# The conditioning stage of a hybrid decoder layer: two row tiles of h per step, 1 KB packets, a ring of weight tiles

## The chip, the cores and the metric

The kernel runs on one core of a Trainium2 chip. The metric is the device time of one execution in microseconds (us). Three runs of the kernel before took 1973.09, 1976.62 and 1977.78 us; the median is 1976.62 us. The engines in the text are PE (TensorE, matrix products; its weight loads are a row of their own, PEld), DVE (VectorE), ACT (ScalarE), POOL (GpSimd) and SP (SyncE), which issues nearly all DMAs here.

## The reference

One decoder layer on x of shape (1024, 2048), in float32. What matters for the change is its beginning:

```
shift, scale, gate = split(silu(c) @ w_ada + b_ada)      # c: (2048,), w_ada: (2048, 6144)
h    = x * (1 + scale) + shift                           # (1024, 2048)
proj = h @ w_in                                          # w_in: (2048, 7184)
... retention (4 heads), gated DeltaNet (8 heads), mixed @ w_out, gate, LayerNorm
```

The first two thirds of w_ada (33.5 MB) and all of x (8.4 MB) have to be read before the last row tile of h exists. The product with w_in is the first large one.

## The kernel before

h is kept transposed, as 16 row tiles (index kt) of 128 channels by 1024 tokens, each split into a high part h_hi and a low part h_lo, both in a reduced float32 format that PE takes at full rate. A product of h and w_in is three products: high by high, low by high, high by low.

The first stage, the conditioning stage, makes the 16 row tiles and does the first of the products meanwhile. It runs in steps s_ (lines 332 to 372). In a step, for row tile kt = s_:

- `load_w` (L188) loads the columns of shift and scale that belong to kt: four tiles `wa` of 256 KB twice, where each packet is 128 floats, 512 bytes. `load_x` (L184) loads the 128 channels of x, also in 512-byte packets.
- `accumulate` (L196) multiplies row r of each partition by silu(c) and adds it up on DVE, 14 rows of 256 elements (shift and scale side by side) into two accumulators that are added at the end (L205). The last two rows are left to PE.
- `reduce` (L207), in the next step, sums over the partitions with PE: products one column wide with the accumulator and the two rows that are left over. DVE adds the bias (`mod`, L219).
- `transpose_x` (L229) turns x on PE in two groups of four transposes, and ACT copies them out of PSUM.
- `modulate` (L216): ACT scales and shifts (L223), ACT rounds to h_hi (L224), DVE subtracts to get h_lo (L227).
- `load_item`, `split_item`, `first_mms` (L243, L266, L277): an item is one row tile of w_in with the columns of a group (0 or 1). It is loaded, split into w_hi (ACT, L274) and w_lo (DVE, L275) and multiplied in three units t = 0, 1, 2. A unit is six products 512 wide (L291), except unit 2 of group 0, six products 272 wide (L286). There are 32 items, 96 units.

A planner (L313 to L328) puts the units into steps and slots. It takes the items in the order of `TURNS` (L142): row tiles 0 to 3 of group 0, 0 to 7 of group 1, 4 to 11 of group 0, 8 to 15 of group 1, 12 to 15 of group 0. A unit of the newest row tile may not stand before slot `LATE`; a step has `SLOTS` slots, a unit counts one slot (0.6 for the short kind), and what does not fit goes to the next step. All engines follow this written order in the stage (`manual_schedule`), and each queue, SP's too, runs strictly in order. When a group's turn ends, its three sums are evicted from PSUM to SBUF, by ACT the first time (L306) and by DVE as an addition later (L308).

Behind the stage come the other products with w_in (`gemm_v`, L489, is the first, `gemm_cm`, L457, the most) with the heads' work between them, and at the end the product with w_out.

Of the kernel before, what the change touches and what calls it, by code (L numbers as in the profile page):

```python
# [58 lines left out]
def hybrid_layer_kernel(ctx: ExitStack, tc: tile.TileContext, x, c, w_ada, b_ada, w_in, gdn_conv_w,  # L59
# [86 lines left out]
    part_g, part_k, part_q0, part_k0, part_g0 = (pa.tile([P, T], F32, name=f"part{i}", tag=f"part{i}")  # L146
                                                 for i in range(5))
    part_v = pa.tile([P, 2, DV + 16], F32, name="part5", tag="part5")
    parts = ((part_g, part_k, part_v), (part_q0, part_k0, part_g0))
    hH, hL = [], []  # L150
    with ExitStack() as st:
# [8 lines left out]
        def load_params():  # L160
            prm = sp.tile([P, P], F32, name="prm", tag="acc", bufs=4)
            nc.sync.dma_start(out=prm[:96], in_=gdn_conv_w[0].rearrange("j (t p) -> (j t) p", p=P))
            nc.sync.dma_start(out=prm[96:128], in_=b_ada[0, :2 * D].rearrange("(t p) -> t p", p=P))
            prm2 = sp.tile([32, P], F32, name="prm2", tag="acc", bufs=4)
# [15 lines left out]
        NV = 14  # L180
        NS = 4
        xss, xTs, accs, was, raws, splits = {}, {}, {}, {}, {}, {}

        def load_x(kt):  # L184
            xss[kt] = sp.tile([P, NC, P], F32, name="xs", tag="xs")
            nc.sync.dma_start(out=xss[kt], in_=x3[:, :, kt * P:(kt + 1) * P])

        def load_w(kt, rhs=range(4)):  # L188
            for rh in rhs:
                wa = sp.tile([P, 4, 2, P], F32, name="wa", tag="wa", bufs=7)  # L190
                for s in range(2):
                    nc.sync.dma_start(out=wa[:, :, s, :], in_=ada3[:, rh * 4:rh * 4 + 4,
                                                                  s * D + kt * P:s * D + (kt + 1) * P])
                was.setdefault(kt, []).append(wa)

        def accumulate(kt, r0, r1):  # L196
            if r0 == 0:
                accs[kt] = [sp.tile([P, 2 * P], F32, name="acc", tag="acc", bufs=4) for _ in range(2)]
            for r in range(r0, r1):
                wr, a = was[kt][r // 4][:, r % 4].rearrange("p s n -> p (s n)"), accs[kt][r % 2]  # L200
                V.scalar_tensor_tensor(out=a, in0=wr, scalar=cs[:, r:r + 1],  # L201
                                       in1=zero.broadcast_to([P, 2 * P]) if r < 2 else a, op0=ALU.mult, op1=ALU.add)
            if r1 == NV:
                a, b = accs[kt]
                V.scalar_tensor_tensor(out=a, in0=a, scalar=1.0, in1=b, op0=ALU.mult, op1=ALU.add)  # L205

        def reduce(kt):  # L207
            a, _ = accs.pop(kt)
            pm = px.tile([P, 512], F32, name="px", tag="px")
            for s in range(2):  # L210
                for r in range(NV, 16):
                    PE.matmul(pm[:, s:s + 1], was[kt][r // 4][:, r % 4, s], cs[:, r:r + 1], start=r == NV, stop=False)
                PE.matmul(pm[:, s:s + 1], a[:, s * P:(s + 1) * P], ones[:, 0:1], start=False, stop=True)
            return pm

        def modulate(kt, pm):  # L216
            xT = xTs.pop(kt)
            mod = sp.tile([P, 2], F32, name="mod", tag="mod")
            V.tensor_tensor(out=mod, in0=pm[:, 0:2], in1=bcol[:, kt], op=ALU.add)  # L219
# [3 lines left out]
            S.activation(out=xT, in_=xT, func=AF.Identity, scale=mod[:, 1:2], bias=mod[:, 0:1])  # L223
# [5 lines left out]
        def transpose_x(kt, i):  # L229
            if i == 0:  # L230
                xTs[kt] = sp.tile([P, T], F32, name="xT", tag="xT")
            ph = px.tile([P, 512], F32, name="px", tag="px")
            for j in range(4):
                PE.transpose(ph[:, j * P:(j + 1) * P], xss[kt][:, 4 * i + j], ident)
            S.copy(xTs[kt][:, i * 512:(i + 1) * 512], ph)
# [7 lines left out]
        def load_item(n):  # L243
# [7 lines left out]
            if grp == 2:  # L251
                r3 = raw[:, :2 * (DV + 16)].rearrange("p (a n) -> p a n", n=DV + 16)
                nc.sync.dma_start(out=r3[:, :, :DV], in_=w3[:, 0:2, RV:RV + DV])
                nc.sync.dma_start(out=r3[:, :, DV:], in_=w3[:, 0:2, GA:GA + 16])
                cols = ()
            elif grp == 0:
                cols = ((RG + P, P), (GK, P), (RV, DV), (GA, 16))
            else:
                cols = ((RQ, P), (RK, P), (RG, P))
# [53 lines left out]
        todo = [(n, t) for n in range(len(items) - 1) for t in range(3)]  # L313
        plan = []
        for s_ in range(KT + 1):
            plan.append([])
            at = 0.0
            while todo and s_:
                n, t = todo[0]
                grp, kt = items[n][:2]  # L320
                if kt == s_ - 1:
                    at = max(at, LATE)
                if kt > s_ - 1 or (s_ < KT and at > SLOTS - 1 + 0.2):
# [5 lines left out]
        load_w(0, range(1))  # L329
        load_x(0)  # L330
        prm = load_params()
        for s_ in range(KT + 1):
            if s_ < KT:
                load_w(s_, range(0 if s_ else 1, 4))
                if s_ < KT - 1:
                    load_x(s_ + 1)
            for n in ((0,), (1, 2))[s_] if s_ < 2 else ():
                load_item(n)
# [4 lines left out]
            if s_ < KT:  # L343
# [5 lines left out]
            if 1 <= s_ <= 3:  # L349
                h_rest()  # L350
            h_rest = None
            for i in range(max([SLOTS] + [e[0] + 1 for e in plan[s_]])):
# [18 lines left out]
                if i == LATE - 1 and h_rest:  # L371
                    h_rest()
# [858 lines left out]
```

## Time and profile before

| | us |
|---|---|
| median of three runs | 1976.62 |
| the profiled execution | 1977.74 |
| its span, from the first to the last instruction | 1976.0 |
| PE busy in the span | 1890.5 (96%) |
| DVE busy | 1154.2 (58%) |
| ACT busy | 554.6 (28%) |
| the first product behind the stage (L489) starts at | 211.76 |

PE's time is busy nearly throughout; the slices in which it is not are at the start. A busy share says nothing of the clock: the granted clock of a stretch (PEclk, 1.00 for 2.4 GHz throughout) stands beside it in the windows. The share of the DMA engines in a stretch can go over 1, since packets overlap.

### The profile page before, as it was taken

What the parts mean: (1) busy time and instruction counts of PE and PEld (TensorE: products, weight loads), DVE (VectorE), ACT (ScalarE), POOL (GpSimd) and SP (SyncE); (2) the same over time, 40 slices, a digit from 0 to 9 for tenths busy, and PEclk for the clock granted to TensorE, in tenths of its full rate; (3) what the DMA queues carried; (4) which work ended last, traced back from release to release, by engine and by line L of the source; (5) the groups of instructions that cost most, each with busy time, mean ns of one, the idle gap of its engine ahead of it and who ended that gap; (6) DMA issues with size and microseconds to landing.
All of it is one profiled execution on the core that took longest, in us unless ns stands there. A gap on an engine that the chain in (4) does not pass through costs nothing.

```text
span 1976.0 us, 28123 instructions
## 1 busy us (share of the span) xinstructions
PE 1890.5 (96%) x10400; PEld 1595.4 (81%) x10400; DVE 1154.2 (58%) x2953; ACT 554.6 (28%) x1243; POOL 168.4 (9%) x165
## 2 busy tenths in 40 slices
PE   5989999999999999999999999999999999998996
PEld 4768888787878888787878898898898878886885
DVE  6767657564765757574665752544542534458557
ACT  3443223332322232322323221211211232234221
POOL 0000101000000000000000000100100100005102
PEclk8999999999999999999999999999999999999998
DMA  9998312222222222221222241144141166345532
GB/s 259 281 255 215 95 54 72 54 73 54 68 59 58 60 57 67 54 71 50 72 54 58 63 139 48 43 145 134 38 139 49 55 209 221 123 136 186 180 112 91
DMA packets 292459, 210.07 MB, mean 106 GB/s; under 512 B 44681, under 2 KB 252122, under 8 KB 291554
## 3 DMA queue, kind: packets, MB, share of 16 engines
q1 hardware_dynamic: 289698, 199.89, 36.1%
q0 software_dynamic: 2624, 8.39, 1.2%
q8 instruction: 81, 1.33, 0.3%
q14 instruction: 56, 0.46, 0.1%
HBM read 189.31 MB, written 18.92 MB: 105 GB/s over the span
## 4 chain that ended last, share of the span: by engine, by line
PE 73%; DMA 4%; DVE 4%; issue 1%; ACT 1%; POOL 1%; SPq 0%; DVEq 0%; ACTq 0%; POOLq 0%
PE pg L457 44%; PE po L1086 15%; PE pg L489 6%; DMA gb<-gc_d 3%; DMA graw<-in_w_ada_dram 1%; PE ps L774 1%; PE ps L933 1%; PE ps L917 1%; PE ps L911 1%; POOL z L1142 1%; PE ps L932 1%; PE ps L923 1%; PE ps L584 1%; PE ps L583 0%; PE ps L574 0%
## 5 line engine op out<-in xcount | busy, mean ns | idle before, releaser
L457 PE MATMUL pg<-h_hi,w_hi 128*128 128x512 f32 x1376 | 451.9, 400 | 0.0
L457 PE MATMUL pg<-h_hi,w_lo 128*128 128x512 f32 x1376 | 449.8, 400 | 0.0
L457 PE MATMUL pg<-h_lo,w_hi 128*128 128x512 f32 x1376 | 448.7, 400 | 0.0
L1086 PE MATMUL po<-wr,ms 128*128 128x512 f32 x1380 | 319.3, 393 | 8.1 <-DVE wr L1033 5.5
L1086 PEld LDWEIGHTS po<-wr,ms 128*128 128x128 f32 x1380 | 260.8, 190 | 64.7 <-DVE wr L1033 7.4
L457 PEld LDWEIGHTS pg<-h_lo,w_hi 128*128 128x128 f32 x1376 | 257.8, 189 | 47.9
L457 PEld LDWEIGHTS pg<-h_hi,w_lo 128*128 128x128 f32 x1376 | 257.4, 189 | 48.1 <-DVE w_lo L95 0.5
L457 PEld LDWEIGHTS pg<-h_hi,w_hi 128*128 128x128 f32 x1376 | 256.6, 189 | 49.0 <-ACT w_hi L94 1.7
L94 ACT CAST w_hi<-w_raw 128x512 fp32r<-128x512 f32 (+1 forms) x203 | 126.1, 621 | 598.2 <-PE pg L457 440.6
L95 DVE TENSOR_TENSOR w_lo<-w_raw,w_hi 128x512 fp32r<-128x512 f32 (+1 forms) x203 | 143.1, 705 | 211.6 <-ACT w_hi L94 206.9
L1033 DVE TENSOR_TENSOR wr<-raw,wr 128x512 fp32r<-128x512 f32 x116 | 88.2, 763 | 111.5 <-ACT wr L1031 108.7
L489 PE MATMUL pg<-w_lo,h_hi 128*128 128x256 f32 (+1 forms) x448 | 128.6, 287 | 2.3 <-DVE w_lo L95 2.3
L489 PE MATMUL pg<-w_hi,h_hi 128*128 128x256 f32 (+1 forms) x448 | 128.9, 288 | 0.4 <-DVE part L308 0.4
L489 PE MATMUL pg<-w_hi,h_lo 128*128 128x256 f32 (+1 forms) x448 | 128.7, 287 | 0.0
L1031 ACT CAST wr<-raw 128x512 fp32r<-128x512 f32 x116 | 71.6, 621 | 158.4 <-PE po L1086 145.8
L647 DVE SCALAR_TENSOR_TENSOR yc<-pg,cw,yc 128x1023 f32<-128x1023 f32 (+2 forms) x69 | 88.3, 1280 | 3.0 <-ACT yc L644 1.9
L489 PEld LDWEIGHTS pg<-w_lo,h_hi 128*128 128x128 f32 x448 | 86.2, 192 | 2.8 <-DVE w_lo L95 2.7
L489 PEld LDWEIGHTS pg<-w_hi,h_hi 128*128 128x128 f32 x448 | 86.2, 192 | 2.5 <-ACT w_hi L94 1.7
L489 PEld LDWEIGHTS pg<-w_hi,h_lo 128*128 128x128 f32 x448 | 86.2, 192 | 0.0
L201 DVE SCALAR_TENSOR_TENSOR acc<-wa,cs,acc 128x256 f32<-128x256 f32 x192 | 82.2, 481 | 4.5 <-DMA wa<-in_w_ada_dram 3.4
L437 DVE SCALAR_TENSOR_TENSOR gacc<-graw,cs,gacc 128x512 f32<-128x512 f32 x60 | 48.7, 811 | 51.5 <-DMA graw<-in_w_ada_dram 51.0
L291 PE MATMUL pg<-h_hi,w_hi 128*128 128x512 f32 x160 | 57.9, 445 | 17.0 <-ACT h_hi L224 14.7
(253 smaller groups left out, 2380.0 us busy)
## 6 DMA issues: line engine op xcount, KB each, us to landing
w_raw<-in_w_in_dram SPq DMA_DIRECT2D x204, 256.0 KB
wa<-in_w_ada_dram SPq DMA_DIRECT2D x128, 256.0 KB
raw<-in_w_out_dram SPq DMA_DIRECT2D x128, 256.0 KB
graw<-in_w_ada_dram SPq DMA_DIRECT2D x64, 256.0 KB
xs<-in_x_dram SPq DMA_DIRECT2D x16, 512.0 KB
gb<-gc_d SPq DMA_DIRECT2D x32, 256.0 KB
raw<-mixed SPq DMA_DIRECT2D x32, 256.0 KB
z<-in_x_dram SPq DMA_DIRECT2D x32, 256.0 KB
```

Source lines behind the costliest of these rows:

```text
L94: S.copy(hi[:, :n], raw[:, :n])
L95: V.tensor_tensor(out=lo[:, :n], in0=raw[:, :n], in1=hi[:, :n].bitcast(F32), op=ALU.subtract)
L201: V.scalar_tensor_tensor(out=a, in0=wr, scalar=cs[:, r:r + 1], in1=zero.broadcast_to([P, 2 * P]) if r < 2 else a, op0=ALU.mult, op1=ALU.add)
L291: PE.matmul(ps0[t][:, i * 512:(i + 1) * 512], w[:, t * P:(t + 1) * P], hh[:, i * 512:(i + 1) * 512], start=(first and w is hi and hh is hH ...
L437: V.scalar_tensor_tensor(out=a, in0=raw[:, :512], scalar=cs[:, r:r + 1], in1=a, op0=ALU.mult, op1=ALU.add)
L457: PE.matmul(pt[:, i * 512:(i + 1) * 512], w[:, kk], hh[:, i * 512:(i + 1) * 512], start=(kt == 0 and w is hi and hh is hH[kt]), stop=(kt = ...
L489: PE.matmul(dsts[tt - tts[0]], hh[:, tsl], w[:, kk], start=(kt == 0 and first_in_bank and hh is hH[kt] and w is hi), stop=(kt == KT - 1 an ...
L584: PE.matmul(po[:, :DV], sc[:, ch], vt[:, ch], start=(ch == 0), stop=True)
L647: V.scalar_tensor_tensor(out=y[:, s:], in0=pt[:, :T - s], scalar=cw[:, j * 24 + ti:j * 24 + ti + 1], in1=y[:, s:], op0=ALU.mult, op1=ALU.add)
L1031: S.copy(t[:, :512], raw)
L1033: V.tensor_tensor(out=t[:, 512:], in0=raw, in1=t[:, :512].bitcast(F32), op=ALU.subtract)
L1086: PE.matmul(pts[tt], m[:, a + tt * P:a + (tt + 1) * P], w, start=(n == 0 and a == 0 and w is wh), stop=(n == KT - 1 and a == 512))
```

## The change

A step now handles a pair of row tiles, 2 pair and 2 pair + 1. There are 8 steps and a last one, where there were 16 and a last one.

- A weight tile `wa` holds 2 rows by shift and scale by 256 columns, where it held 4 rows by 128 columns. It has the same bytes and the same two DMAs; a packet is 1 KB. There are still 7 buffers and 64 tiles.
- `load_w` has no step any more: it is called behind every use and issues the next tiles whose buffers' old contents are used up, in order (a ring).
- x comes as four token tiles by 256 channels, with 1 KB packets, still 512 KB each, issued in slots 7 and 10.
- `accumulate` works on 512 elements at a time and on 15 rows (`NV`), where there were 14 of 256; PE's `reduce` has one row left over, and gives shift and scale of two row tiles at once.
- `SLOTS` is 12; `LATE` is 4 for the first row tile of the pair and 5 for the second.
- The columns RG (2 P wide: g0 and g1) of w_in are one load in group 1; the first retention head's key columns RK go to group 0 in exchange for the one half of RG.

The planner's units by step were 3, 3, 3, 3, 6, 6, 6, 6, 7, 7, 7, 3, 6, 6, 6 and 18 for steps 1 to 16. They are 6, 9, 12, 11, 14, 11, 12 and 21 for steps 1 to 8.

The core of the diff:

```diff
-    SLOTS, SLOT, LATE = 6, 1.38, 3
+    COLS = (((RK, P), (GK, P), (RV, DV), (GA, 16)), ((RQ, P), (RG, 2 * P)))
+    SLOTS, LATE = 12, (4, 5)
...
-        NV = 14
+        NV = 15
         NS = 4
...
-        def load_w(kt, rhs=range(4)):
-            for rh in rhs:
-                wa = sp.tile([P, 4, 2, P], F32, name="wa", tag="wa", bufs=7)
+        def load_x(pair, i):
+            xss[pair, i] = sp.tile([P, 4, 2 * P], F32, name="xs", tag="xs")
+            nc.sync.dma_start(out=xss[pair, i], in_=x3[:, 4 * i:4 * i + 4, pair * 2 * P:(pair + 1) * 2 * P])
+
+        def load_w():
+
+            while len(was) < 4 * KT and (len(was) < NB or len(was) - NB in used):
+                pair, r = len(was) // 8, len(was) % 8 * 2
+                wa = sp.tile([P, 2, 2, 2 * P], F32, name="wa", tag="wa", bufs=NB)
                 for s in range(2):
...
         def accumulate(pair, r0, r1):
             if r0 == 0:
+                accs[pair] = [sp.tile([P, 4 * P], F32, name=f"acc{i}", tag=f"acc{i}", bufs=2 - i) for i in range(2)]
             for r in range(r0, r1):
+                wr, a = was[8 * pair + r // 2][:, r % 2].rearrange("p s n -> p (s n)"), accs[pair][r % 2]
...
+                if r % 2:
+                    used.add(8 * pair + r // 2)
...
+            load_w()
...
             if s_ == 1:
                 lo0 = split_item(0)
-            if 1 <= s_ <= 3:
-                h_rest = modulate(s_ - 1, reduce(s_ - 1))
-            if s_ < KT:
+                mod = reduce(0)
+                for kt in range(2):
+                    modulate(kt, mod)()
+            if s_ < NP:
                 accumulate(s_, 0, NS)
...
+                if s_ > 1:
+                    if i == 0:
+                        mod = reduce(s_ - 1)
+                    if i in (0, 2):
+                        h_rests.append(modulate(2 * s_ - 2 + i // 2, mod))
+                if s_ < NP and i < SLOTS:
                     accumulate(s_, NS + i * (NV - NS) // SLOTS, NS + (i + 1) * (NV - NS) // SLOTS)
-                    if i in (1, 3):
-                        transpose_x(s_, i // 2)
+                    if i in (5, 6, 8, 9):
+                        transpose_x(s_, i // 8, (i - 5) % 3)
+                    if i in (7, 10) and s_ < NP - 1:
+                        load_x(s_ + 1, i // 8)
...
+                if s_ > 1 and i in (2, 4):
+                    h_rests.pop(0)()
```

How the written order moves is shown at three places. On DVE, at the start of the first step that has an h, before (acc is the accumulator of the weight rows, mod the shift and scale, w_lo the low part of the first item, h_lo that of the first row tile):

```order
L205 SCALAR_TENSOR_TENSOR acc<-acc 128x256
L219 TENSOR_TENSOR mod<-px,bcol 128x2
L201 SCALAR_TENSOR_TENSOR acc<-wa,cs,zero 128x256 x2
L201 SCALAR_TENSOR_TENSOR acc<-wa,cs,acc 128x256 x2
L275 TENSOR_TENSOR w_lo<-w_raw,w_hi 128x528
L227 TENSOR_TENSOR h_lo<-xT,h_hi 128x1024
L201 SCALAR_TENSOR_TENSOR acc<-wa,cs,acc 128x256 x6
```

And now, at the same place on DVE:

```order
L214 SCALAR_TENSOR_TENSOR acc_159<-acc_159,acc_160 128x512
L231 TENSOR_TENSOR mod<-px,bcol 128x4
L245 TENSOR_TENSOR h_lo<-xT,h_hi 128x1024 x2
L208 SCALAR_TENSOR_TENSOR acc_277<-wa,cs,zero 128x512
L208 SCALAR_TENSOR_TENSOR acc_278<-wa,cs,zero 128x512
L208 SCALAR_TENSOR_TENSOR acc_277<-wa,cs,acc_277 128x512
L208 SCALAR_TENSOR_TENSOR acc_278<-wa,cs,acc_278 128x512
L291 TENSOR_TENSOR w_lo<-w_raw,w_hi 128x528
```

The low parts of both row tiles stand ahead of the next weight rows, and w_lo of the first item behind four of them. On PE, the first reduction and what stands around it, before (xs is x as loaded, px a PSUM tile, pg the sums of the units):

```order
L234 MATMUL px<-ident,xs 128x128 x8
L212 MATMUL px<-cs,wa 128x1 x2
L213 MATMUL px<-ones,acc 128x1
L212 MATMUL px<-cs,wa 128x1 x2
L213 MATMUL px<-ones,acc 128x1
L234 MATMUL px<-ident,xs 128x128 x4
L291 MATMUL pg_260<-h_hi,w_hi 128x512 x2
```

And now:

```order
L252 MATMUL px<-ident,xs 128x128 x16
L224 MATMUL px<-cs,wa 128x1
L226 MATMUL px<-ones,acc_159 128x1
L224 MATMUL px<-cs,wa 128x1
L226 MATMUL px<-ones,acc_159 128x1
L224 MATMUL px<-cs,wa 128x1
L226 MATMUL px<-ones,acc_159 128x1
L224 MATMUL px<-cs,wa 128x1
L226 MATMUL px<-ones,acc_159 128x1
L307 MATMUL pg_304<-h_hi,w_hi 128x512 x2
```

Eight narrow products serve two row tiles, where six served one. On DVE, the start of the step after that, now:

```order
L214 SCALAR_TENSOR_TENSOR acc_277<-acc_277,acc_278 128x512
L208 SCALAR_TENSOR_TENSOR acc_402<-wa,cs,zero 128x512
L208 SCALAR_TENSOR_TENSOR acc_403<-wa,cs,zero 128x512
L208 SCALAR_TENSOR_TENSOR acc_402<-wa,cs,acc_402 128x512
L208 SCALAR_TENSOR_TENSOR acc_403<-wa,cs,acc_403 128x512
L231 TENSOR_TENSOR mod<-px,bcol 128x4
L208 SCALAR_TENSOR_TENSOR acc_402<-wa,cs,acc_402 128x512
L208 SCALAR_TENSOR_TENSOR acc_403<-wa,cs,acc_403 128x512
L245 TENSOR_TENSOR h_lo<-xT,h_hi 128x1024
```

From the second step on, four weight rows stand ahead of mod and two more between mod and h_lo. Behind the stage the order is as it was on every engine but for one half of a silu product, which stands one row earlier on DVE.

## Rows read from the trace of the kernel before

**Rows 1.** The page's first line: the span and all instructions.

```profile
span 1976.0 us, 28123 instructions
```

**Rows 2.** Windows: stretch, its length, busy us (instructions) per engine, PEclk, DMA share, GB/s.

```profile
12.00:53.00 41.00, 28.26 (x130) 23.26 (x130) 28.48 (x64) 12.30 (x16) 0.00 (x0) 0.88 1.06 277
53.00:118.00 65.00, 60.91 (x323) 50.99 (x323) 50.26 (x113) 31.55 (x42) 0.00 (x0) 0.97 1.02 268
118.00:157.00 39.00, 30.88 (x154) 25.08 (x155) 26.73 (x57) 13.15 (x18) 0.00 (x0) 0.87 1.01 272
157.00:211.80 54.80, 54.66 (x286) 45.92 (x285) 37.22 (x74) 19.50 (x28) 0.00 (x0) 1.00 0.69 180
```

**Rows 3.** Timeline (start, us, engine, line): last mod, first product behind the stage.

```profile
190.55 0.16 DVE L219 TENSOR_TENSOR mod<-px,bcol 128x2 f32<-128x2 f32 x1 [3.74 <-PE px L213]
...
211.76 0.28 PE L489 MATMUL pg<-w_hi,h_hi 128*128 128x272 f32 x1
```

**Rows 4.** PE's largest wait in the whole stage: us, times, longest.

```profile
PE pg L291 <- ACT h_hi L224: 14.7, 6, 4.2
```

**Rows 5.** The page's DMA issues that the stage makes: count, KB each.

```profile
w_raw<-in_w_in_dram SPq DMA_DIRECT2D x80, 64.0 KB
w_raw<-in_w_in_dram SPq DMA_DIRECT2D x16, 128.0 KB
...
wa<-in_w_ada_dram SPq DMA_DIRECT2D x128, 256.0 KB
...
xs<-in_x_dram SPq DMA_DIRECT2D x16, 512.0 KB
```

**Rows 6.** DMA in the stretch 50 to 65 us, 512-byte packets, queue never empty.

```profile
DMA packets 8935, 4.43 MB, mean 295 GB/s; under 512 B 289, under 2 KB 8935, under 8 KB 8935
```

**Rows 7.** DMA in the stretch 1637 to 1646 us, 2 KB packets, queue full.

```profile
DMA packets 1920, 3.50 MB, mean 389 GB/s; under 512 B 217, under 2 KB 217, under 8 KB 1919
```

**Rows 8.** PE's timeline late in the stage: reduction, units, transposes, short units.

```profile
157.40 0.50 PE L212 MATMUL px<-cs,wa 128*128 128x1 f32 x4
...
158.90 0.71 PE L291 MATMUL pg<-h_hi,w_hi 128*128 128x512 f32 x2
...
160.71 0.71 PE L291 MATMUL pg<-h_hi,w_hi 128*128 128x512 f32 x2
...
162.19 0.62 PE L291 MATMUL pg<-h_hi,w_hi 128*128 128x512 f32 x2
...
163.57 0.60 PE L234 MATMUL px<-ident,xs 128*128 128x128 f32 x4
...
200.47 0.28 PE L286 MATMUL pg<-w_hi,h_hi 128*128 128x272 f32 x1
...
201.22 0.63 PE L291 MATMUL pg<-h_hi,w_hi 128*128 128x512 f32 x2
```

**Rows 9.** Groups of 0 to 230 us on DVE: busy us, mean ns of one.

```profile
L201 DVE SCALAR_TENSOR_TENSOR acc<-wa,cs,acc 128x256 f32<-128x256 f32 x192 | 82.2, 481 | 4.5 <-DMA wa<-in_w_ada_dram 3.4 <-DVE mod L219 0.7
...
L275 DVE TENSOR_TENSOR w_lo<-w_raw,w_hi 128x528 fp32r<-128x528 f32 (+2 forms) x33 | 20.9, 632 | 12.6 <-ACT w_hi L274 9.7 <-DMA w_raw<-in_w_in_dram 2.8
...
L227 DVE TENSOR_TENSOR h_lo<-xT,h_hi 128x1024 fp32r<-128x1024 f32 x16 | 19.6, 1223 | 2.2 <-ACT h_hi L224 2.1
```

**Rows 10.** The same operation 512 wide, behind the stage: ns min/median/max.

```profile
L437 DVE SCALAR_TENSOR_TENSOR gacc<-graw,cs,gacc x60: 747/752/1754, 1142.0 to 1471.7; 128x512 f32<-128x512 f32 x60
```

**Rows 11.** Timeline of the start: last weight row added, mod, first unit.

```profile
15.52 0.42 DVE L205 SCALAR_TENSOR_TENSOR acc<-acc 128x256 f32<-128x256 f32 x1
...
17.90 0.16 DVE L219 TENSOR_TENSOR mod<-px,bcol 128x2 f32<-128x2 f32 x1 [1.96 <-PE px L213]
...
20.53 1.22 PE L291 MATMUL pg<-h_hi,w_hi 128*128 128x512 f32 x2 [1.71 <-ACT h_hi L224]
```

**Rows 12.** Two products 512 wide behind a wait of PE, and 5 us later.

```profile
34.07 1.22 PE L291 MATMUL pg<-h_hi,w_hi 128*128 128x512 f32 x2 [2.17 <-ACT h_hi L224]
...
39.19 0.63 PE L291 MATMUL pg<-h_lo,w_hi 128*128 128x512 f32 x2
```

More of the change, by code (lines that the diff above doesn't have):

```diff
@@ L160, in load_params @@
         def load_params():
[L161 removed]
+            prm = sp.tile([P, P], F32, name="prm", tag="xT")
             nc.sync.dma_start(out=prm[:96], in_=gdn_conv_w[0].rearrange("j (t p) -> (j t) p", p=P))
             nc.sync.dma_start(out=prm[96:128], in_=b_ada[0, :2 * D].rearrange("(t p) -> t p", p=P))
[L164 removed]
+            prm2 = sp.tile([32, P], F32, name="prm2", tag="xT")
             V.memset(prm2, 0.0)
@@ L196, in accumulate @@
-        def accumulate(kt, r0, r1):
+        NB = 7
+        xss, xTs, accs, raws, splits = {}, {}, {}, {}, {}
+        was, used = [], set()
+        def load_x(pair, i):
[5 more added lines that the diff above has]
+                wa = sp.tile([P, 2, 2, 2 * P], F32, name="wa", tag="wa", bufs=NB)
+                for s in range(2):
+                    nc.sync.dma_start(out=wa[:, :, s, :], in_=ada3[:, r:r + 2, s * D + pair * 2 * P:
+                                                                  s * D + (pair + 1) * 2 * P])
+                was.append(wa)
+                if len(was) == 1:
+                    return
@@ L197, in accumulate @@
+        def accumulate(pair, r0, r1):
             if r0 == 0:
-                accs[kt] = [sp.tile([P, 2 * P], F32, name="acc", tag="acc", bufs=4) for _ in range(2)]
+                accs[pair] = [sp.tile([P, 4 * P], F32, name=f"acc{i}", tag=f"acc{i}", bufs=2 - i) for i in range(2)]
             for r in range(r0, r1):
-                wr, a = was[kt][r // 4][:, r % 4].rearrange("p s n -> p (s n)"), accs[kt][r % 2]
+                wr, a = was[8 * pair + r // 2][:, r % 2].rearrange("p s n -> p (s n)"), accs[pair][r % 2]
@@ L209, in reduce @@
+        def reduce(pair):
+            a, _ = accs.pop(pair)
             pm = px.tile([P, 512], F32, name="px", tag="px")
[L210 to L216, printed above, removed]
+            for i in range(2):
+                for s in range(2):
+                    o, sl = 2 * i + s, slice(i * P, (i + 1) * P)
+                    for r in range(NV, 16):
+                        PE.matmul(pm[:, o:o + 1], was[8 * pair + r // 2][:, r % 2, s, sl], cs[:, r:r + 1],
+                                  start=r == NV, stop=False)
+                    PE.matmul(pm[:, o:o + 1], a[:, (2 * s + i) * P:(2 * s + i + 1) * P], ones[:, 0:1],
+                              start=False, stop=True)
+            used.add(8 * pair + 7)
+            load_w()
+            mod = sp.tile([P, 4], F32, name="mod", tag="mod")
+            V.tensor_tensor(out=mod, in0=pm[:, 0:4], in1=bcol[:, 2 * pair:2 * pair + 2].rearrange("p k s -> p (k s)"),
+                            op=ALU.add)
+            return mod
@@ L217, in modulate @@
+        def modulate(kt, mod):
             xT = xTs.pop(kt)
-            mod = sp.tile([P, 2], F32, name="mod", tag="mod")
-            V.tensor_tensor(out=mod, in0=pm[:, 0:2], in1=bcol[:, kt], op=ALU.add)
+            i = kt % 2 * 2
             pool = hx if kt < 2 else hp
@@ L222, in modulate @@
             h_lo = pool.tile([P, T], F32R, name="h_lo", tag="h")
-            S.activation(out=xT, in_=xT, func=AF.Identity, scale=mod[:, 1:2], bias=mod[:, 0:1])
+            S.activation(out=xT, in_=xT, func=AF.Identity, scale=mod[:, i + 1:i + 2], bias=mod[:, i:i + 1])
             S.copy(h_hi, xT)
@@ L313, in hybrid_layer_kernel @@
         todo = [(n, t) for n in range(len(items) - 1) for t in range(3)]
+        NP = KT // 2
         plan = []
-        for s_ in range(KT + 1):
+        for s_ in range(NP + 1):
             plan.append([])
@@ L328, in hybrid_layer_kernel @@
         assert not todo
-        load_w(0, range(1))
-        load_x(0)
+        h_rests = []
+        load_w()
+        load_x(0, 0)
         prm = load_params()
-        for s_ in range(KT + 1):
-            if s_ < KT:
[L334 to L338, printed above, removed]
+        load_w()
+        load_x(0, 1)
+        for s_ in range(NP + 1):
             if s_ == 1:
                 lo0 = split_item(0)
-            if 1 <= s_ <= 3:
-                h_rest = modulate(s_ - 1, reduce(s_ - 1))
-            if s_ < KT:
+                mod = reduce(0)
+                for kt in range(2):
+                    modulate(kt, mod)()
+            if s_ < NP:
                 accumulate(s_, 0, NS)
```

45 lines of the change are left out of this document (14 added, 31 removed).

## The prediction

> **What bounds the kernel now.** I read the page first, then windows over the first 300 us, then PE's waits, DVE's and PE's timelines and the DMA by stretch. The page gives a span of 1976.0 us [rows 1], with 1.74 us around it in the profiled execution (1977.74). The stage ends where the first product behind it starts, at 211.76 us [rows 3]; the 1764 us behind are not touched, and the order there is as it was. So the question is when that product starts.
>
> The stage has two faces in the windows [rows 2]. From 12 to 53 and from 118 to 157 us PE is busy 28.3 of 41 and 30.9 of 39 us, at a granted clock of 0.88 and 0.87, while the DMA share is 1.06 and 1.01: loading sets the pace. From 53 to 118 us PE is busy 60.9 of 65, and from 157 us to the end 54.7 of 54.8 at full clock: there PE is the bound. What PE waits for most is h_hi, 14.7 us in six waits [rows 4], that is, the weights of the next row tile and the chain behind them. PE's work at full clock can be added up from rows: a unit takes 1.38 us (162.19 to 163.57), a short unit 0.75 (200.47 to 201.22), a group of transposes about 0.45 (158.90 to 160.71 less a unit), a reduction 1.50 (157.40 to 158.90) [rows 8]. 80 units, 16 short ones, 32 groups and 16 reductions are 110.4 + 12 + 14.4 + 24 = 160.8 us. So of 211.8 us some 51 are waits, slow clock and the start.
>
> **DMA.** A 256 KB transfer of 512 packets takes 0.889 us at 295 GB/s [rows 6], one of 128 packets of 2 KB takes 0.674 us at 389 GB/s [rows 7]. In between the trace shows nothing saturated, so 256 packets of 1 KB are bounded by 0.674 and 0.889 us; I take a fixed cost per packet, (0.889 - 0.674) / 384 = 0.56 ns, which puts 1 KB at 0.746 us, 351 GB/s. The counts [rows 5]: 128 transfers of wa and 16 of xs (twice the size) cost 128 x 0.889 + 16 x 1.778 = 142 us and will cost 119. The items' loads are 80 of 64 KB, 16 of 128 KB and small ones, about 25 us; with g0 and g1 as one, 48 and 32, about 24. The floor of all loading falls from 168 to 144 us, 18 per pair.
>
> The Trainium skill, "DMA: Bandwidth & Descriptors", Specifications, puts the smallest transfer for line rate at 512 B, so by it 1 KB would gain nothing. The two stretches, 295 against 389 GB/s with full queues, disagree with it. By the page the loading floor would stay at about 167 us; that result is rival B.
>
> **PE.** Units and transposes are the same. A reduction has 8 narrow products for two row tiles where it had 12, so 2.0 us a pair instead of 3.0: 8 us less in all, 152.8 us. Where PE is the bound this counts in full.
>
> **DVE.** A row of 256 takes 0.48 us and is 0.42 apart from the next (192 rows in 82.2 us busy) [rows 9]; a row of 512 takes 0.75 [rows 10], so about 0.69 apart. A pair had 28 + 2 of the first, 12.6 us, and gets 15 + 1 of the second, 11.0. With two h_lo (1.22 each) and four w_lo (0.63) [rows 9] a pair costs 16.1 us, and 3 more in a step with evictions. That is below PE's 20, so it costs nothing while DVE does not wait. But it waits: it reaches h_lo 1.4 us behind mod (two rows), and the h_hi it needs comes 2.6 us behind mod (17.90 to 20.53) [rows 11]. About 1.2 us there and half as much at w_lo makes 17.9.
>
> **The start gets later.** Now mod comes at 17.90 us. The first pair needs 4.2 MB of wa and 1.05 MB of x, 15 us at 351 GB/s behind some 3 us of start, so the last tile lands near 18.4; a row and the sum are 1.5 us; eight narrow products behind a wait, at half clock, are some 3.5 us (from the end of the sum to mod, the six of before took 1.96 [rows 11]). First mod: 23.5, first unit 26.1. Its second product needs w_lo of item 0, and the order shows what is ahead of that on DVE: both h_lo (to 29.6, since ACT makes the second h_hi 2.3 us behind the first) and four rows (2.8), so PE stands until 33. This is an added wait. All of DVE's rows of pair 1 are behind it: 15 rows, the sum and three w_lo are 13 us, so they end near 43.5, and the second mod is at 47.5 (four rows of the next pair stand ahead of it, PE's reduction beside them). Meanwhile PE has 7.0 us of units, no bound. The seven buffers cover about 11 us of loading, so the DMA stops for at most 2 us.
>
> **The steps.** In step 2 PE waits for h until 50.1 (47.5 + 2.6), then has 11.2 us of units and 1.8 of transposes. Behind a wait a pair of products takes 1.22 us and some 5 us later 0.63 [rows 12], the two levels of 1.2 and 2.4 GHz, so about 2.2 us are lost to the clock; then a unit and the reduction, 3.4: third mod at 68.7 (DVE alone 47.5 + 17.9 + 2 = 67.4). From here every step has units of older row tiles to start with, which cover the 2.6 us to h, and PE sets the pace: units, 1.8, 2.0. Step 3: 20.4; 4: 19.0; 5: 20.0; 6: only 17.1, but DVE with two evictions and the reduction needs about 20; 7: 20.4. The sum, 99.8 us, gives a last mod at 168.5. Before, steps 5 to 8 took 11.0 us a row tile against 10.7 worked out in this way, so I add 2.8 us. Behind the last mod 20 of the last step's 21 units follow, 25.1 us; the two of row tile 13 ahead of the new ones cover the chain to h. (The same reckoning gives 20.9 for before; the rows show 211.76 - 190.55 = 21.2 [rows 3].) The stage ends at 168.5 + 2.8 + 25.1 = 196.4, 15.4 us earlier than now.
>
> The span is then 1960.6 and the execution 1962.3; on the scale of the median, 1976.62 - 15.4 = **1961**.
>
> Bounds: if the start is 1.5 us earlier, step 1 takes 20, step 2 DVE's 17.5, step 6 PE's 17.1 and nothing is added, the end is 22 + 20 + 17.5 + 97 + 25.1 = 181.6, a gain of 30 us (1946). At the other end 512-byte rates and half-clock stretches in steps 1, 2 and 6 leave 4 us (1973).
>
> **Rivals.**
> A. The forecast: PE takes over from the third mod; 1961.
> B. The packets are no faster, or the change does not do what it says to the rate. Then pair 0 lands 2.8 us later, and steps 1 to 7 need 17.8 us for wa and x and 1.8 to 4.2 for items, 144 us in sum; with 5% of waits the end is 26.3 + 151 + 25.1 = 203, a gain of 9: 1968. For it: no stretch shows 1 KB packets in a full queue. Against: the two rates that are shown differ by a third.
> C. The gain is given back behind the stage: 1976. For it: nothing that I can name; PE is busy there almost without a break, and what loads there is far from full.
> D. Slower: the coupling on DVE's queue in step 1 (mod, both h_lo, then rows, then sum, then reduction) repeats in every step. Its price is the 24 us of step 1: seven times that behind 23.5 is 191.5, the stage ends at 217, and with PE's waits of over 4 us at half clock, 1.7 us a step, at 228: 1976.62 + 16 = 1993, or 1982 without the clock. It decides from 23.3 us a step on, where the last mod comes later than 211.8 - 25.1 = 186.7. Against it: from step 2 on the order puts four rows ahead of mod and two ahead of h_lo, and PE has older units from step 3 on.
> E. Better: DVE and clock cost nothing, 1950.
>
> **Chances.** A 0.62, B 0.15, C 0.09, D 0.06, E 0.08. The measurement can tell 0.3%, 5.9 us, from no change. Faster by more than that (below 1970.7) are A, E and four fifths of B: 0.82. Within it are C and the rest of B: 0.12. Slower, D: 0.06. The range from 1950 to 1973 leaves out C and D and about half of E.
>
> **What would show it.** Right: wa transfers at 340 to 360 GB/s while the queue is full; the first unit near 26 us with a hole on PE to 33; third mod near 68, PE busy above 95% at full clock from there to the end, the first product of gemm_v near 196, and what is behind it 1764 us long. Wrong: rates below 310 GB/s (B); periods of mod above 22 us from step 3 on, with DVE waiting for h_hi or for PE's reduction (D); or PE's waits behind the stage grown by more than 3 us (C).

## The result and the profile after

The changed kernel took 1965.76 us (median of 4 runs, 1962.76 to 1967.61) beside 1976.86 us of the kernel before on the same chip: a ratio of 0.9946 with an interval of [0.9928, 0.9964], 11.1 us less. Later executions of the same kernel gave 0.9927 [0.9910, 0.9944], 14.0 us less. The forecast, 1961 us and a ratio of 0.992, lies just outside the first interval and inside the second.

The page after, beside [rows 1]:

```profile
span 1963.2 us, 27906 instructions
...
PE 1875.3 (96%) x10336; PEld 1584.3 (81%) x10336; DVE 1143.9 (58%) x2833; ACT 555.0 (28%) x1243; POOL 170.4 (9%) x165
```

DVE now sums the weight rows, answering to [rows 9], in these (busy us, mean ns of one, idle before):

```profile
L208 DVE SCALAR_TENSOR_TENSOR acc<-wa,cs,acc 128x512 f32<-128x512 f32 x104 | 73.3, 746 | 5.5 <-DMA wa<-in_w_ada_dram 5.1
```

The windows over the stage, cut at the first unit (28.6 us) and near the third, fifth and seventh mod, answer to [rows 2]. The last row is the whole stage.

```profile
core 0: us, PE busy (x) PEld busy (x) DVE busy (x) ACT busy (x) POOL busy (x), PEclk, DMA share, GB/s
0.00:28.60 28.60, 8.35 (x34) 6.92 (x34) 12.54 (x27) 6.76 (x10) 0.20 (x4) 1.00 0.90 281
28.60:70.70 42.10, 32.84 (x161) 27.19 (x162) 32.58 (x48) 16.75 (x23) 0.00 (x0) 0.92 1.03 329
70.70:110.70 40.00, 39.94 (x209) 33.22 (x209) 30.90 (x47) 20.40 (x27) 0.00 (x0) 1.00 0.95 299
110.70:150.30 39.60, 37.80 (x209) 32.22 (x209) 34.44 (x49) 18.09 (x24) 0.00 (x0) 0.96 1.00 315
150.30:195.66 45.36, 45.30 (x224) 37.64 (x224) 25.22 (x35) 17.78 (x25) 0.00 (x0) 1.00 0.42 118
0.00:195.66 195.66, 164.23 (x834) 137.19 (x835) 135.69 (x204) 79.78 (x108) 0.20 (x4) 0.97 0.85 264
```

The same row of the kernel before:

```profile
0.00:211.76 211.76, 177.27 (x899) 147.10 (x899) 147.13 (x323) 79.12 (x108) 0.20 (x4) 0.94 0.92 244
```

The two last rows say where the 16.1 us came from. PE is busy 13.0 us less (177.27 to 164.23) and idle only 3.1 us less (34.5 to 31.4). By lines of the kernel, the narrow products of the reductions were busy 30.3 us (18.28 on L212, 12.04 on L213) and are now 24.4 (11.94 on L224, 12.43 on L226), 6.0 less. The 480 wide products of the units went from 133.6 to 126.9, 6.7 less, and the transposes from 22.5 to 20.9. (Products overlap at their ends, so the parts add up to a little more than 13.0.) The wide products are the same ones, so their part is one of pace. The mean granted clock went from 0.94 to 0.97; 0.06 of 211.8 and 0.03 of 195.7 us are, as an estimate, 6.8 us of full clock regained. From 70.7 us on PE is busy 123.0 of 125.0 us. Its waits behind 70.7 us fell from 8.8 to 1.9 us, and those of the first 28.6 us rose from 15.4 to 20.3: waiting went to the start of the stage, and there is nearly as much of it as there was.

PE's timeline: the first unit, the hole behind it, the two later waits, and the last reduction (start, duration, engine, line, operation; in brackets the idle time before it and what ended it).

```profile
28.65 1.22 PE L307 MATMUL pg<-h_hi,w_hi 128*128 128x512 f32 x2 [2.66 <-ACT h_hi L242]
35.40 1.22 PE L307 MATMUL pg<-h_hi,w_lo 128*128 128x512 f32 x2 [5.53 <-DVE w_lo L291]
...
51.99 1.22 PE L307 MATMUL pg<-h_hi,w_hi 128*128 128x512 f32 x2 [3.41 <-ACT h_hi L242]
...
132.55 1.22 PE L307 MATMUL pg<-h_hi,w_hi 128*128 128x512 f32 x2 [1.80 <-ACT h_hi L242]
...
168.47 0.28 PE L224 MATMUL px<-cs,wa 128*128 128x1 f32 x2
...
170.18 0.71 PE L307 MATMUL pg<-h_hi,w_hi 128*128 128x512 f32 x2
```

A reduction for two row tiles takes 1.71 us (168.47 to 170.18). One of before, for one row tile, takes 1.26, from its first narrow product to the unit behind it:

```profile
168.13 0.50 PE L212 MATMUL px<-cs,wa 128*128 128x1 f32 x4
...
169.39 0.71 PE L291 MATMUL pg<-h_hi,w_hi 128*128 128x512 f32 x2
```

So do 13 of the 16; the 1.50 us of [rows 8] is one of three longer ones. Two row tiles thus cost 2.52 us and now 1.71, 0.8 us less a pair and 6.5 us in all by these late rows at full clock.

DVE's timeline: the last row and the sum of pair 0, and then five of the eight mods.

```profile
21.31 0.75 DVE L208 SCALAR_TENSOR_TENSOR acc<-wa,cs,acc 128x512 f32<-128x512 f32 x1 [1.55 <-DMA wa<-in_w_ada_dram]
22.09 0.69 DVE L214 SCALAR_TENSOR_TENSOR acc<-acc,acc 128x512 f32<-128x512 f32 x1
...
26.02 0.16 DVE L231 TENSOR_TENSOR mod<-px,bcol 128x4 f32<-128x4 f32 x1 [3.24 <-PE px L226]
...
49.37 0.15 DVE L231 TENSOR_TENSOR mod<-px,bcol 128x4 f32<-128x4 f32 x1
...
70.69 0.16 DVE L231 TENSOR_TENSOR mod<-px,bcol 128x4 f32<-128x4 f32 x1 [1.35 <-PE px L226]
...
90.75 0.16 DVE L231 TENSOR_TENSOR mod<-px,bcol 128x4 f32<-128x4 f32 x1 [1.35 <-PE px L226]
...
170.35 0.16 DVE L231 TENSOR_TENSOR mod<-px,bcol 128x4 f32<-128x4 f32 x1 [4.00 <-PE px L226]
```

The DMA in a stretch where the queue is full (53 to 63 us), beside [rows 6] and [rows 7]:

```profile
DMA packets 3773, 3.49 MB, mean 349 GB/s; under 512 B 237, under 2 KB 3773, under 8 KB 3773
```

So packets of 1 KB came at 349 GB/s. The forecast, interpolated between 295 and 389, was 351. The Trainium skill ("DMA: Bandwidth & Descriptors", Specifications) puts the smallest transfer for line rate at 512 B; the trace disagrees, since 512 B gives 295 and 1 KB 349 in full queues of the same stage.

### The profile page after: what moved, and what is told of

Read it like the earlier page. It is cut to its first block, busy times and chain, and to the rows that moved or that the text cites. A ratio compares the mean times of both kernels' runs of the same rounds, so it can differ in the third digit from the quotient of the medians.

```text
span 1963.2 us, 27906 instructions
## 1 busy us (share of the span) xinstructions
PE 1875.3 (96%) x10336; PEld 1584.3 (81%) x10336; DVE 1143.9 (58%) x2833; ACT 555.0 (28%) x1243; POOL 170.4 (9%) x165
## 4 chain that ended last, share of the span: by engine, by line
PE 72%; DMA 6%; DVE 4%; issue 1%; POOL 1%; ACT 1%; SPq 0%; DVEq 0%; ACTq 0%; POOLq 0%
PE pg L476 44%; PE po L1105 14%; PE pg L508 6%; DMA gb<-gc_d 4%; DMA raw<-mixed 1%; DMA graw<-in_w_ada_dram 1%; PE ps L793 1%; POOL z L1161 1%; PE ps L936 1%; PE ps L930 1%; DVE et L755 1%; PE ps L952 1%; PE ps L603 1%; PE ps L951 1%; POOL yc L917 0%
## 5 line engine op out<-in xcount | busy, mean ns | idle before, releaser
L1050 ACT CAST wr<-raw 128x512 fp32r<-128x512 f32 x116 | 71.6, 621 | 157.0 <-PE po L1105 148.4
L208 DVE SCALAR_TENSOR_TENSOR acc<-wa,cs,acc 128x512 f32<-128x512 f32 x104 | 73.3, 746 | 5.5 <-DMA wa<-in_w_ada_dram 5.1
```

What stands on the lines that cost most here:

```text
L1050: S.copy(t[:, :512], raw)
```

## The experiments

Ratios are to the kernel before on the same chip. "The stage ends" means the first product of gemm_v; with the changed kernel that is 195.66 us. Times are the median of all executions of a kernel, while mods, waits and the end of the stage come from the one execution that was profiled. What the ring of `load_w` is worth by itself was not tested.

**Smaller packets, first try.** Each transfer of wa and xs is cut by columns into two of 512 B packets.

```diff
-  nc.sync.dma_start(out=wa[:, :, s, :], in_=ada3[:, r:r + 2, 256 columns])
+  for k in range(2): nc.sync.dma_start(out=wa[:, :, s, k * P:(k + 1) * P], in_=ada3[:, r:r + 2, 128 columns])
```

> The changed kernel with every transfer of wa and x cut into two of half the columns, so that all packets are 512 bytes again; tiles, order and 512-wide products stay. Theory (the packets set the loading rate, 0.889 us per 256 KB against 0.75): full stretches run at 290 to 300 GB/s, a pair costs 20 us or more of loading, mod comes every 20.5 to 22 us and the stage ends 5 to 9 us later, at 201 to 205 us instead of 195.7. Rival (the gain comes from the wide products and the shorter reductions, packets do not matter): the stage ends at 195 to 198 us. The transfers are also twice as many; the run beside it shows what that alone costs.

Ratio 1.0087 [1.0070, 1.0103], 1997.12 us; the stage ends at 231.3, far behind the 201 to 205 expected. That is slower than the kernel before, which has such packets too. The edit changed two things, the packets and the number of transfers, and the next run tells them apart.

**As many transfers, packets of 1 KB.** The same cut by rows.

```diff
+  for k in range(2): nc.sync.dma_start(out=wa[:, k, s, :], in_=ada3[:, r + k, 256 columns])
```

> The control: also twice as many transfers of half the size, but cut by rows, so that packets stay 1 KB. Theory (size of the packet, not the count of transfers): 340 to 355 GB/s in full stretches, the stage ends within 2 us of 195.7. Rival (SP's issuing of more transfers is what costs): it ends as late as the run with 512-byte packets, at 201 us or later.

Ratio 1.0058 [1.0036, 1.0081], 1990.64 us; the stage ends at 222.9. I had expected the number of transfers to cost next to nothing, and it costs 27 us of the stage. SP's timeline shows a run of such issues, start and length:

```profile
62.85 8.03 SPq L201 DMA_DIRECT2D wa<-in_w_ada_dram  x16
```

and of the changed kernel:

```profile
70.46 4.04 SPq L197 DMA_DIRECT2D wa<-in_w_ada_dram  x8
```

In both stretches one issue takes 0.50 us (8.03 / 16, 4.04 / 8), at 128 as at 256 KB. With 256 KB that is over 500 GB/s, no limit; with 128 KB it is 261 GB/s, below what the packets allow. The DMA of this kernel from 60 to 80 us agrees:

```profile
DMA packets 6223, 5.59 MB, mean 279 GB/s; under 512 B 639, under 2 KB 6223, under 8 KB 6223
```

From 20 to 180 us SP waited for a DMA only 6.4 us here, which speaks for SP's own issuing as the limit; but single issues took 0.33 to 1.6 us, and why they differ the trace does not show. The first run is therefore no test of the packet size; the next two are.

**Packets of 512 B and of 1 KB with equal transfers.** Both kernels have tiles of four weight rows in three buffers and load each by four transfers of 256 KB, as large as those of the change; in one they are cut by columns (512 B), in the other by rows (1 KB).

```diff
-  NB = 7
+  NB = 3
-  wa = sp.tile([P, 2, 2, 2 * P], F32, name="wa", tag="wa", bufs=NB)
+  wa = sp.tile([P, 4, 2, 2 * P], F32, name="wa", tag="wa", bufs=NB)
+  (512 B) nc.sync.dma_start(out=wa[:, :, s, k * P:(k + 1) * P], in_=ada3[:, r:r + 4, 128 columns])
+  (1 KB)  nc.sync.dma_start(out=wa[:, 2 * k:2 * k + 2, s], in_=ada3[:, r + 2 * k:r + 2 * k + 2, 256 columns])
```

> 512-byte packets for wa without more transfers: a weight tile holds 4 rows by shift and scale by 256 columns in three buffers (where there were 7 of 2 rows), and comes in four transfers of 256 KB, 4 rows by 128 columns each, as many as the changed kernel issues. x keeps 1 KB packets. To be read against the next run, which differs in the packets alone. Theory (packet size sets the rate as long as SP keeps up): wa at 290 to 300 GB/s, 0.14 us more per transfer, 128 of them 18 us of loading, of which the PE-bound steps hide a part: the stage ends 5 to 12 us later than in the next run. Rival (count of transfers was all that mattered): within 2 us of the next run.

> The control for the run before it: the same tiles of 4 rows in three buffers, in four transfers of 256 KB, 2 rows by 256 columns each, packets of 1 KB. Both theories: 340 to 355 GB/s in full stretches; the coarser ring costs 0 to 6 us, so the stage ends at 195 to 202 us.

With 512 B: 0.9968 [0.9955, 0.9981], 1973.64 us, the stage ends at 208.5. With 1 KB: 0.9930 [0.9905, 0.9955], 1965.32 us, at 197.7. The packet size of wa alone is 10.8 us of the stage in the profiled executions. It is 8.3 us in the medians: the profiled 512 B execution, 1977.08 us, is one of the slowest of its ten (1970.14 to 1977.66). The difference lies where loading sets the pace (the third mod comes at 75.4 and 70.7 us) and not from the third to the fifth, where PE does (39.95 and 40.00 us). The DMA with full queues, of the 512 B kernel (50 to 65 us):

```profile
DMA packets 8230, 4.40 MB, mean 294 GB/s; under 512 B 275, under 2 KB 8230, under 8 KB 8230
```

and of the 1 KB kernel (53 to 60 us):

```profile
DMA packets 2612, 2.44 MB, mean 349 GB/s; under 512 B 165, under 2 KB 2612, under 8 KB 2612
```

So with 512 B packets of wa the rest of the change (the cheaper reductions, the fewer rows of DVE, the 1 KB packets of x) is worth some 3 us (211.8 to 208.5), for then loading sets the pace. The coarser ring of these kernels costs about 2 of it (197.7 against 195.66 with 1 KB).

**Half as many transfers.** As the 1 KB kernel, with two transfers of 512 KB a tile.

```diff
+  nc.sync.dma_start(out=wa[:, :, s], in_=ada3[:, r:r + 4, 256 columns])
```

> The same tiles of 4 rows, but two transfers of 512 KB each: half as many wa transfers, packets of 1 KB. Theory A (SP's issuing, 0.47 to 0.6 us a transfer whatever its size, still holds back the changed kernel in its first 70 us): the stage ends 2 to 5 us earlier than in the run before. Theory B (at 256 KB a transfer SP is no bound any more, the engines are): within 1.5 us of the run before.

0.9917 [0.9897, 0.9938], 1963.53 us; the stage ends at 196.2, 1.5 us before that of the four transfers. The ratios don't tell the two apart, so from 256 KB on the number of transfers is worth 1.5 us or nothing.

**One more row tile's product on PE.** The sum over weight rows leaves two of 16 to PE instead of one: four more narrow products a pair (12 instead of 8), and one row less on DVE.

```diff
-  NV = 15
+  NV = 14
```

> The changed kernel with 14 rows on DVE instead of 15, so that PE has two rows left over: 12 narrow products per pair instead of 8, as many as before. Theory (PE sets the pace from the third mod on, the reduction counts in full): 1.0 us more per step in steps 3 to 7 and some in the last reduction, the stage ends 4 to 7 us later, at 200 to 203 us. Rival (loading or DVE sets the pace in these steps, with PE just filling its time): the stage ends within 1.5 us of 195.7, since DVE has a row less.

0.9963 [0.9949, 0.9976], 1971.33 us; the stage ends at 204.9, 9.2 us later. The stage gets longer when DVE gets less to do, and from the third to the fifth mod PE is busy 41.63 of 41.70 us: PE is the bound there. But the size is above the 4 to 7 us expected. The windows of this kernel:

```profile
71.50:113.20 41.70, 41.63 (x225) 34.99 (x225) 29.64 (x44) 20.39 (x27) 0.00 (x0) 1.00 0.91 283
113.20:156.10 42.90, 41.10 (x225) 35.16 (x225) 33.13 (x47) 17.97 (x24) 0.00 (x0) 0.91 0.95 296
156.10:204.90 48.80, 48.80 (x232) 40.90 (x233) 24.60 (x34) 17.77 (x25) 0.00 (x0) 0.93 0.38 104
```

The first stretch, at full clock, shows 0.85 us more a step (41.70 for two, where the change has 40.00), near the 1.0 expected. In the last PE is busy throughout and yet takes 3.4 us more than 45.36, of which one reduction explains 0.9, at a mean granted clock of 0.93: the excess lies where the clock is below its upper level. What brought it down there, with PE busy throughout, is open. A reduction of this kernel takes 2.60 us:

```profile
175.75 0.51 PE L224 MATMUL px<-cs,wa 128*128 128x1 f32 x4
...
178.35 0.71 PE L307 MATMUL pg<-h_hi,w_hi 128*128 128x512 f32 x2
```

That is as much as two reductions of six narrow products before (2.52). What the change saves on PE is thus the four products, and not that two reductions became one.

**The split of weights ahead of the first h_lo.** In step 1 the four rows of the next pair and the split of item 0 are put ahead of mod, to fill the hole of 5.5 us and let DVE go on.

```diff
+  if s_ == 1:
+      lo0 = split_item(0)
       lo0()
+      mod = reduce(0)
+      for kt in range(2): modulate(kt, mod)()
```

(behind the first four rows of pair 1; the lines with a plus are taken out ahead of them)

> The changed kernel with only the start of step 1 reordered on DVE: four rows of pair 1 and w_lo of the first item stand ahead of mod and of both h_lo, as in later steps. Theory (DVE's order at the start sets the second mod, and PE's work sets the steps from the third on, so that an earlier start moves all behind it): PE's wait of 5.5 us for w_lo is gone, DVE's waits of 3.2, 2.4 and 1.0 us are filled, the second mod comes 4 to 6.5 us earlier than 49.4 and the stage ends 3.5 to 6.5 us earlier, at 189 to 192 us. Rival (loading, at a share of 0.95 to 1.03 in these steps, is what paces them): the second mod moves, but the stage ends at 194 us or later.

0.9933 [0.9918, 0.9948], 1964.53 us; the stage ends at 197.1, 1.4 us later. The second mod does come earlier, at 46.97 instead of 49.37. The third does not: 71.72 against 70.69, and 69.20 in the repetition below. PE's waits gave the reason, first its timeline and then the waits of ACT and DVE from 27 to 72 us (in total, times, longest):

```profile
65.40 0.73 PE L307 MATMUL pg<-h_hi,w_hi 128*128 128x512 f32 x2 [2.39 <-ACT part L322]
```

```profile
DVE acc L208 <- DMA wa<-in_w_ada_dram: 4.3, 4, 1.3
ACT w_hi L290 <- DMA w_raw<-in_w_in_dram: 3.9, 1, 3.9
```

DVE and ACT now wait for the DMA, and an eviction queued behind ACT's cast holds PE. So DVE's order sets the second mod: step 1, from the first mod to the second, takes 19.6 us here instead of 23.35, while packets of 512 B and of 1 KB left it the same in the two kernels above (22.6 and 22.5). But what step 1 wins step 2 loses (24.75 us instead of 21.32), and that step goes with the loading: 23.5 with 512 B and 20.9 with 1 KB. So the theory that an earlier second mod moves all behind it fell, and closing the hole on PE was worth nothing.

**g0 and g1 as two loads again**, with the column groups of the kernel before.

```diff
-  COLS = (((RK, P), (GK, P), (RV, DV), (GA, 16)), ((RQ, P), (RG, 2 * P)))
+  COLS = (((RG + P, P), (GK, P), (RV, DV), (GA, 16)), ((RQ, P), (RK, P), (RG, P)))
```

> One part undone: the groups of columns are the old ones (one half of RG in group 0, RK in group 1, three loads of 64 KB per item of group 1). Theory (the third eviction behind the silu product of g1 is what makes the first products behind the stage wait): the stage ends at 195 to 197 us, PE's wait for the eviction is 0.4 us again instead of 1.4, and the stretch from the stage's end to the first product of gemm_cm is 41.3 to 42.5 us long instead of 43.4. Rival (the 2 us lost there have nothing to do with the groups): it stays at 43 us or more.

0.9924 [0.9909, 0.9939], 1963.53 us. The stage ends at 197.6, 2.0 us later (195 to 197 were expected), and what is behind it takes 1760.9 us instead of 1767.5 (and 1766.0 in the repetition below). The profiled execution, 1960.29 us, is the fastest of its six, so not all of that is the edit. Of it 2.1 us are found in gemm_v: from its first product to the first of gemm_cm 43.5 us in the changed kernel, 41.3 here and 41.4 before. PE's waits there (190 to 245 us) in the changed kernel:

```profile
PE pg L508 <- DVE w_lo L95: 3.4, 2, 2.7
PE pg L508 <- DVE part L324: 1.4, 1, 1.4
```

and with the old groups:

```profile
PE pg L508 <- DVE w_lo L95: 2.3, 2, 2.1
PE pg L508 <- DVE part L324: 0.4, 1, 0.4
```

DVE's timeline at the end of the changed stage shows why: one half of the silu of g (L534) stands between the evictions for which PE waits. With the old groups the three evictions follow one another, as the last line, of that kernel, shows.

```profile
193.74 1.22 DVE L324 SCALAR_TENSOR_TENSOR part<-pg,part 128x1024 f32<-128x1024 f32 x1
194.88 0.68 DVE L534 SCALAR_TENSOR_TENSOR sg<-th,part 128x512 f32<-128x512 f32 x1
195.48 1.22 DVE L324 SCALAR_TENSOR_TENSOR part<-pg,part 128x1024 f32<-128x1024 f32 x1
...
197.24 0.72 DVE L324 SCALAR_TENSOR_TENSOR part<-pg,part 128x544 f32<-128x544 f32 x1
```

```profile
195.63 3.23 DVE L324 SCALAR_TENSOR_TENSOR part<-pg,part 128x1024 f32<-128x1024 f32 x3
```

The two waits are 4.8 us together in all eleven profiled executions with the new groups, whose stretch is 41.9 to 44.7 us long at a mean granted clock from 1.00 down to 0.92, and 2.7 in the three with the old ones (41.3 to 41.4 us at 0.96). The one load thus wins 2 us in the stage and loses them directly behind it, and the ratios with and without it (0.9927 in the repetition below, 0.9924) don't tell the two apart.

**The changed kernel again**, without an edit.

> The changed kernel once more, unchanged, in the same call: its ratio to the kernel before with more rounds, and how much the 1767.5 us behind the stage vary from one execution to another. Theory (the 3.3 us lost behind the stage are mostly an effect of the order): the stage ends within 0.5 us of 195.7 and what is behind it takes 1766 to 1769 us. Rival (they are chance): it takes 1764 or less, or over 1770.

0.9927 [0.9910, 0.9944], 1964.38 us; the first mod (25.79), the seventh (150.16), the last (170.2) and the stage's end (195.5) agree with the first profile within 0.3 us. The mods between come up to 1.5 us earlier (the third at 69.2), and step 6 gives that back.

**The small parameter loads later**, behind the first seven weight tiles, to give those the queue.

```diff
-  prm = load_params()          (ahead of the first weights)
+  prm = load_params()          (behind them; used in slot 4 of step 0)
```

> The changed kernel with the five small loads of parameters issued behind the first seven weight tiles, where they stood behind the first one, and used in slot 4. Theory (from the first transfer to the third mod the loading decides, and SP spends 2.3 us on the small ones while nothing else is under way): the first mod comes 2 to 2.5 us earlier (23.5 to 24), and so do the third mod (68 to 68.7) and the end of the stage (193 to 193.8). Rival (DVE's and ACT's order sets the first steps): the first mod comes earlier, the third and the end by less than 0.7 us.

0.9915 [0.9896, 0.9934], 1963.72 us, no slower than the changed kernel (0.9927). But the profiled execution, 1966.85 us and the slowest of its six, has the first mod 2.7 us later, at 28.71, and the stage's end 2.1 later, at 197.8. SP's issues and the rate of the DMA from 0 to 25 us (40 equal slices):

```profile
3.16 9.35 SPq L197 DMA_DIRECT2D wa<-in_w_ada_dram  x12
12.90 0.34 SPq L163 DMA_DIRECT2D prm<-in_gdn_conv_w_dram  x1
...
15.91 0.22 SPq L169 DMA_DIRECT2D prm<-in_gdn_norm_w_dram  x1
```

```profile
GB/s 1 0 11 105 110 279 300 234 216 283 298 262 300 356 362 372 351 356 347 347 349 347 349 346 315 185 95 57 97 270 326 336 331 295 277 333 361 380 360 337
```

In this program each transfer that SP issues waits for the one eight before it, and SP's waits show each of the five small ones held by a transfer of wa, 0.4 to 0.5 us each. Five small transfers among them (12.9 to 16 us) by that leave room for three large ones under way, and the rate falls to 57 GB/s near 17 us. The expectation missed. What this execution does show is a delay at the start that comes through nearly whole: of 2.7 us 2.1 are left at the end.

**The small loads by POOL.**

```diff
-  nc.sync.dma_start(out=prm[:96], ...)
+  nc.gpsimd.dma_start(out=prm[:96], ...)
```

(and the four others alike)

> The changed kernel with the five small loads of parameters issued by POOL instead of SP, in the same place. Moving them behind the weight tiles made the first mod 2.7 us later and the end of the stage 2.1 us later, since each of them then stood between large transfers. Theory (a shift of the first loads is carried to the end of the stage nearly in full): SP's large transfers follow each other from 1.7 us on, the first mod comes 1.5 to 2.5 us earlier than 26.0, the third by as much (68.2 to 69.2), and the stage ends at 193 to 194.2 us. Rival (only delays are carried, a lead is lost again to DVE's and ACT's order as in the run with the rows first): the first mod is earlier, the end within 0.7 us of 195.6.

0.9923 [0.9907, 0.9939], 1963.52 us. The first mod comes at 25.63, 0.4 us earlier, and the stage ends at 196.2, 0.5 later: nothing won, as the rival had it. SP begins earlier and is then held up longer, as its first issues show, of this kernel

```profile
3.16 8.98 SPq L197 DMA_DIRECT2D wa<-in_w_ada_dram  x12
```

and of the changed one:

```profile
5.20 7.59 SPq L197 DMA_DIRECT2D wa<-in_w_ada_dram  x12
```

**A version of what the runs favoured:** 512 KB transfers, the old column groups, the small loads by POOL (the three edits above together).

> Three of the edits together: parameters from POOL, the old groups of columns (three loads per item of group 1), and weight tiles of 4 rows in transfers of 512 KB. Theory: a lead of 2 us at the start and half the weight transfers on SP pay for the 16 more loads of items, so the stage ends at 194 to 196.5 us, and the first products behind it wait as little as with the old groups (41.3 us instead of 43.4): 1.5 to 3 us faster than the changed kernel, a ratio near 0.991. Rival (what is won in the stage is given back behind it whatever the groups): no faster than the changed kernel, 43 us again.

0.9910 [0.9895, 0.9926], 1960.93 us, the lowest median of all. The stage ends at 197.3, behind the 194 to 196.5 expected, and 1760.5 us follow; the first products behind it take the 41.4 us of the old groups. Its interval overlaps that of the changed kernel, so that it is better is likely and not shown.

## Why the prediction was right

```
                        forecast   measured (us)
1 KB packets, GB/s      351        349
first mod               23.5       26.02
hole on PE ends         33         35.40
second, third mod       47.5, 68.7 49.37, 70.69
steps 3 to 7            99.8       99.66 (20.06 19.93 19.24 20.38 20.05)
addition from before    2.8        none needed
last mod                171.3      170.35
tail behind it          25.1       25.31
stage ends              196.4      195.66
behind it               1764       1767.5, 1766.0
```

- **Which theory.** A is what happened: packets faster, PE the bound from the third mod on, busy 39.94 of 40.0 us at full clock and 123.0 of 125.0 to the end. B was priced too low: the kernel with 512 B packets of wa ends its stage at 208.5, some 2 of it for its ring, where 203 was worked out. D's coupling happened once and not again, as the order had said.
- **The start.** Its mechanism was right, the chain mod, h_lo, rows, w_lo and a hole of 5.5 us, but it came 2.5 us late. I let the queue run at 351 GB/s from 3 us on; it moved 281 GB/s over the first 28.6 us, and the last row of pair 0 began at 21.31 with its tile forecast for 18.4. The steps after it took 23.35 (24.0 forecast) and 21.32 (21.2). DVE's queue was rightly named as what sets step 1. But it was not what sets the third mod: with that queue relieved, step 2 lost what step 1 won.
- **The steps.** Their sum is right to 0.2 us, but in part by errors that cancel: each reduction took 0.3 us less than was put down, step 4 0.9 us more. Step 6 came out at 20.4 us, near the 20 that were put down, but not because of DVE. DVE had the sum for the next pair ready at 147.2, and PE's reduction began at 148.4. PE waited 1.80 us for h_hi at 132.55, which the units of older row tiles should have covered (two short ones did not), and ran at a mean granted clock of 0.92 in that step. The 2.8 us added because before ran longer than worked out were not needed. So that the stage's end came out within 0.8 us is partly luck: a start too early by 2.5 and an addition too large by 2.8 cancel.
- **PE.** The 3.0 us of a pair's two reductions before were read from one that took 1.50; the usual 1.26 makes 2.52. Now a pair takes 1.71, not 2.0. So the reductions saved 0.8 us a pair and not 1.0, and 6.0 us of PE's busy time where 8 were forecast. The 6.7 us that the wide products gained by their pace were not in this term; the forecast counted the clock in step 2 alone.
- **Behind the stage.** Here the working failed: "the 1764 us behind are not touched, and the order there is as it was" is 3.3 us off in the first profile. I read the new column groups for what they save in loads (they do, 2 us) and not for what they move on DVE at the stage's end, although the row that moves there had been seen, and rival C named no cause. About 2 us are that swap; the rest lies within what the runs vary by there, 1762 to 1768 us over the kernels with the new groups. Of the 16.1 us that the stage got shorter 12.8 are left between the two profiled executions, and the medians differ by 11.1 and 14.0, where 15.4 was forecast.

## What to carry to other kernels

When a load-bound stage is relieved, add up the next engine's work step by step: the gain here ended where PE's own sum began, and what shortened PE's work came through. Where a transfer's size and its number change together, test each alone; here transfers of half the size cost 27 us and packets of half the size 8 to 11. And a regrouping that pays inside a stage is to be followed to the first waits behind its end.

## What the hardware showed that was not expected

- In full stretches an issue on SP took 0.50 us for 128 and for 256 KB. With transfers of 128 KB the loading moved 232 to 279 GB/s with 1 KB packets and 222 to 269 with 512 B ones, in stretches of 20 us from 20 to 180 us.
- Full queues moved 294 to 295 GB/s with 512 B packets, 346 to 349 with 1 KB and 389 with 2 KB [rows 7]. The same section of the Trainium skill ("DMA: Bandwidth & Descriptors", Specifications) lists about 358 GB/s as the memory's limit per core, half of a stack's 716; here the one core that the kernel runs on moved 389 over 9 us.
- Five small transfers among large ones on one queue let the rate fall from about 347 to 57 GB/s, and of the 2.7 us lost 2.1 were still missing at the end of the stage.
- The granted clock that a window gives does not tell all of PE's pace at the start. From 36.4 to 39.8 us of the changed kernel PE ran nine products in 3.40 us of busy time, as slowly as from 53.0 to 56.4 us, but only the second stretch shows the lower level (PEclk 1.00 and 0.50):

```profile
36.40:39.80 3.40, 3.40 (x9) 2.53 (x8) 3.40 (x6) 0.00 (x0) 0.00 (x0) 1.00 1.04 336
53.00:56.40 3.40, 3.40 (x9) 2.64 (x8) 3.19 (x5) 1.67 (x3) 0.00 (x0) 0.50 1.09 354
```

What slowed the first stretch is not shown.
